# A decoder layer on one core: the second up pair's first product moved behind the first pair's, its weights' sums moved in front of the last output tiles, a later load of the fifth mixed values, and named PSUM banks

## The chip, the cores and the metric

The kernel runs on one core of a Trainium2 chip. The metric is device time in microseconds; the figure for a kernel is the median of its runs. All times in the profile are counted from the start of the span.

TensorE (PE) does the matrix products and loads their stationary operand (PEld, which overlaps). VectorE (DVE) and GpSimd (POOL) do elementwise work, ScalarE (ACT) casts, copies and activations, SyncE (SP) issues the DMAs from one queue, in order.

## The reference

One layer on 1024 positions of width 1024, in float32. Eight heads of sliding-window attention with sinks and eight heads of forgetting attention read the same normalised input; their outputs, side by side, are the mixed values.

```python
mixed = jnp.concatenate([out_a, out_b], axis=-1)       # 1024 x 1024
x = x + jnp.einsum('bse,ed->bsd', mixed, w_out)        # h
hn = rmsnorm(x, mlp_norm_g)
hid = jnp.square(jax.nn.relu(jnp.einsum('bsd,df->bsf', hn, w_up)))   # 4096 wide
x = x + jnp.einsum('bsf,fd->bsd', hid, w_down)
```

## The kernel before

Every float32 product is made of three products in the fast format, of a high and a low part of each operand: high by high, high by low, low by high (`mm`, line 73). `split` makes the parts: a cast on ACT (L77), and the rest by a subtraction on DVE or POOL (L80).

The stages follow each other on PE: input projections and both kinds of attention (to about 430 us, with the first half of the output projection mixed into the tail of attention), the second half of the output projection (`po`, to 468 us), the up product (`pu`, to about 783 us), the down product (`pd`, to the end).

**Output projection.** There are eight output tiles `dt` of 128 columns. Each sums over eight blocks `e` of mixed values. `out_first(dt)` does `e` 0 to 3 while attention still runs and stores the sum with x in DRAM (`part_d`). Once `mix4` to `mix7` are there, `e` 4 to 7 follow: tiles 0 and 4 first, `ahead_of` in the code, partly between the last attention units; then 1, 5, 2, 6, 3, 7. `out_finish(dt)` loads the stored part, adds it on DVE (L981, `h`), stores h, and makes from it slice k = dt % 4 of the seven left operands of the up product: `bh[n]` (high, ACT) and `bl[n]` (low, DVE). The last step of attention, on `mtb`, writes `mix7` in place (L748 and the split of it); `mix3` to `mix6` are loaded from DRAM (L860), one megabyte each.

**Up product.** It is done by pairs `j` of 128-row blocks of w_up, 16 in all, in a scheme of the Strassen kind: seven products per pair instead of eight, in the order `UP = (1, 2, 3, 6, 7, 5, 4)`. Product n of a pair is 12 matmuls: for each k from 0 to 3, wh by `bh[n]`, wh by `bl[n]`, wl by `bh[n]`. Its weights are `wu`, the split of a block of the raw weights (`wur`) or of one of four sums of blocks (`wus`, DVE, L1041 and L1044). For n = 1 the raw block itself is used. For n in (2, 6, 5) DVE makes the low part of `wu`, for the others POOL. Both `bl[n]` for k = 3 and the first pair's `wu` stand on DVE's queue round 470 us.

The code for the order is written as a program in sequence; a scheduler orders each engine's instructions from it, with marks such as `issue_after(x)` (not before x has been issued). SBUF places are named slots ("m3", "r1", "w4"); a new tile in a slot waits until the readers of the old one are done. In front of the up stage,

```python
for dt in (1, 5, 2, 6, 3, 7):
    w = out_weights(dt, 4)
    ps = [bank(f"po{c}") for c in range(2)]
    out_products(ps, w, range(4, 8))
    out_finish(dt, ps)
    if dt == 5:
        with tc.issue_after(part["load"].ins):
            up_load(0)
up_load(1)
```

so the raw weights of pair 0 are issued after the load of tile 5's part, and those of pair 1 behind all tiles.

Of the kernel before, what the change touches and what calls it, by code (L numbers as in the profile page):

```python
# [8 lines left out]
F32 = mybir.dt.float32  # L9
# [7 lines left out]
P = 128  # L17
D = 1024
S = 1024
KT = D // P  # L20
# [35 lines left out]
def hybrid_layer(  # L56
# [15 lines left out]
    def mm(out, lhsT, rhs, start, stop):  # L72
        return nc.tensor.matmul(out, lhsT, rhs, start=start, stop=stop)  # L73
# [70 lines left out]
    def slot(tag, name, shape, dt=F32, pool=None):  # L144
        pool = o[pool or ("zx" if tag in ("w5", "w6") else "zw" if tag[0] == "w" else "zl")]
        return pool.tile([P] + shape, dt, tag=tag, name=name, bufs=1)
# [663 lines left out]
    def heads_b(p):  # L810
        for u in range(8):
            qp, h = (ORDER_END if p == 3 and u > 3 else ORDER_B)[u % 4], u // 4
            unit(lambda: scores_b(p, qp, h), lambda got, qp=qp, h=h: mix_b(got, p, qp, h))
            if u == 1:
                load_c(p, 1)
            if u == DEPTH:
                prep(prep_v, p, 1)
                if p:
                    prep(inverse_to, 6 + 2 * p, dn_b[(p - 1) % 2], 2)
                else:  # L820
                    prep(inverse_a)
            for step in [st.pop(0) for st in splitting if st]:
                step()
            if (p, u) in SPLITS:
                splitting.append(split_mix(SPLITS.index((p, u))))
                splitting[-1].pop(0)()
            if (p, u) in ((2, 4), (3, 1)):
                load_mix(p + 2)
            ahead(p + 1, u)
            fill()  # L830

# [20 lines left out]
        m = mixt[e] = slot(MIX[e], f"mix{e}", [2, S], F32R)  # L852
        mh[e], ml[e] = m[:, 0, :], m[:, 1, :]

    loads = []

    def load_mix(e):
        mix_tiles(e)
        with tc.issue_after(loads[-1]) if e == 4 else nullcontext():
            ld = nc.sync.dma_start(mixt[e].bitcast(F32), mixs_d[e].rearrange("c p s -> p c s"))  # L860
        loads.append(ld.ins)

    nout = [0]

    def out_weights(dt, e0):
        i = nout[0] = nout[0] + 1
        wr = o["zw"].tile([P, 4, P], F32, tag="wor", name="wor", bufs=2)
        nc.sync.dma_start(wr, w_o[dt][:, e0 : e0 + 4, :])
        w = slot(f"w{i % 2}", "wos", [2, 4, P], F32R)
        split(w[:, 0], w[:, 1], wr, nc.scalar, nc.gpsimd)  # L870
        return w[:, 0], w[:, 1]
# [12 lines left out]
    def out_products(ps, w, es):  # L884
        wh, wl = w
        for e in es:
            j = e % 4
            for c in range(2):
                cs = slice(c * 512, (c + 1) * 512)
                mm(ps[c], wh[:, j, :], mh[e][:, cs], j == 0, False)  # L890
                mm(ps[c], wh[:, j, :], ml[e][:, cs], False, False)
            for c in range(2):
                cs = slice(c * 512, (c + 1) * 512)
                mm(ps[c], wl[:, j, :], mh[e][:, cs], False, j == 3)

    def first_banks():
        return [o["pm0"].tile([P, 512], F32, tag=f"m{c}", name=f"po{c}") for c in range(2)]

    def out_first(dt):
        xt = slot(f"w{2 + dt % 2}", "xt", [S])  # L900
        nc.sync.dma_start(xt, xT[dt * P : (dt + 1) * P, :])
        w = out_weights(dt, 0) if dt else first.pop()
        ps = first_banks()
        with paced():
            out_products(ps, w, range(4))
        t = slot("w4", "pc", [S])
        for c in range(2):
            cs = slice(c * 512, (c + 1) * 512)
            nc.scalar.copy(t[:, cs], ps[c])
            nc.gpsimd.tensor_tensor(out=xt[:, cs], in0=xt[:, cs], in1=t[:, cs], op=ALU.add)  # L910
        nc.sync.dma_start(part_d[dt], xt)
# [13 lines left out]
    for p in range(4):  # L925
        heads_b(p)
    fill(True)
    load_mix(6)

    ahead_of = []  # L930
    for dt in (0, 4):
# [43 lines left out]
    def out_finish(dt, ps):  # L975
        t, gain = dt % 4, gm[:, dt : dt + 1]
        h = slot(f"w{2 + dt // 4}", "h", [S]) if dt < 7 else rr
        with tc.issue_after(part["load"].ins) if dt == 7 else nullcontext():
            part["load"] = nc.sync.dma_start(h, part_d[dt])
        for c, cs in enumerate((left, right)):  # L980
            nc.vector.tensor_tensor(out=h[:, cs], in0=ps[c], in1=h[:, cs], op=ALU.add)  # L981
        nc.sync.dma_start(h_d[dt], h)
        if dt < 4:
            h_split(1, t, h[:, left], gain)
            ts = part["t"] = slot("r1", "ts", [4, 512])
            b12 = part["b12"] = slot("w4", "b12", [512])
            nc.scalar.activation(b12, h[:, right], AF.Copy, scale=gain)
            nc.vector.scalar_tensor_tensor(
                out=ts[:, 0], in0=h[:, left], scalar=gain, in1=b12, op0=ALU.mult, op1=ALU.subtract
            )  # L990
            return
        ts, b12 = part["t"], part["b12"]
        h_split(2, t, h[:, left], gain)
        h_split(3, t, h[:, right], gain)
        for i, q, other, op in (
            (1, right, ts[:, 0], ALU.add),
            (2, right, b12, ALU.subtract),
            (3, left, ts[:, 1], ALU.subtract),
        ):
            nc.vector.scalar_tensor_tensor(  # L1000
                out=ts[:, i], in0=h[:, q], scalar=gain, in1=other, op0=ALU.mult, op1=op
            )
        part["rest"] = lambda: sum_splits(ts, t, ((0, 5), (3, 4)))
        sum_splits(ts, t, ((1, 6), (2, 7)))
        if t < 3:
            part.pop("rest")()
# [2 lines left out]
        for i, n in which:  # L1009
            split(bh[n][:, t], bl[n][:, t], ts[:, i], nc.scalar, nc.vector)  # L1010

    for dt, ps, w in ahead_of:
        out_finish(dt, ps)
    pda.close()
    psa.close()
    pm = ctx.enter_context(tc.tile_pool(name="pm", bufs=1, space=PSUM, reuse_waits="tile"))
    bank = lambda name: pm.tile([P, 512], F32, tag="m", name=name, bufs=8)
    raws, up_loads = {}, {}

    def up_load(j):  # L1020
        raws[j] = slot({0: "m3", 1: "m4"}.get(j, f"r{j % 2}"), "wur", [2, KT, P])
        for i in range(2):
            up_loads[j] = nc.sync.dma_start(raws[j][:, i], w_u[j + i * NJ])

    for dt in (1, 5, 2, 6, 3, 7):
        w = out_weights(dt, 4)
        ps = [bank(f"po{c}") for c in range(2)]
        out_products(ps, w, range(4, 8))
        out_finish(dt, ps)
        if dt == 5:  # L1030
            with tc.issue_after(part["load"].ins):
                up_load(0)
    up_load(1)

    def minus(out, a, b, eng=nc.vector):  # L1040
        eng.tensor_tensor(out=out, in0=a, in1=b, op=ALU.subtract)  # L1041
# [1 line left out]
    def plus(out, a, b, eng=nc.vector):  # L1043
        eng.tensor_tensor(out=out, in0=a, in1=b, op=ALU.add)  # L1044

    nw = [4]

    def w_slot(name, shape, dt=F32):
        nw[0] = (nw[0] + 1) % NW
        return slot(f"w{nw[0]}", name, shape, dt)  # L1050

    def up(j):
        if 0 < j < NJ - 1:
            up_load(j + 1)
        raw = raws.pop(j)
        s = slot("m5" if j % 2 == 0 else "m4" if j > 1 else "r1", "wus", [4, 4, P])
        a11, a12, a21, a22 = raw[:, 0, :4], raw[:, 0, 4:], raw[:, 1, :4], raw[:, 1, 4:]
        plus(s[:, 0], a21, a22)  # L1060
        minus(s[:, 1], s[:, 0], a11)
        minus(s[:, 2], a11, a21)
        minus(s[:, 3], a12, s[:, 1])
        src = {1: a11, 2: a12, 3: s[:, 3], 4: a22, 5: s[:, 0], 6: s[:, 1], 7: s[:, 2]}
        m = {}
        for n in UP:
            w = w_slot("wu", [2, 4, P], F32R)
            split(w[:, 0], w[:, 1], src[n], nc.scalar, nc.vector if n in (2, 6, 5) else nc.gpsimd)
            m[n] = bank(f"pu{n}")
            for k in range(4):  # L1070
                mm(m[n], w[:, 0, k], bh[n][:, k], k == 0, False)
                mm(m[n], w[:, 0, k], bl[n][:, k], False, False)
                mm(m[n], w[:, 1, k], bh[n][:, k], False, k == 3)
            if n == 2 and j == 0:
                part.pop("rest")()
            if n == 1:
                u = slot("m1", "u", [4, 512])
                b = slot("m2", "hb", [4, 512])
                nc.scalar.copy(u[:, 0], m[1])
            if n == 2:  # L1080
                plus(b[:, 0], m[2], u[:, 0])
            if n == 6:
                plus(u[:, 1], m[6], u[:, 0])
            if n == 7:
                plus(u[:, 2], m[7], u[:, 1])
# [283 lines left out]
```

## Time and profile before

| | us |
|---|---|
| median of 3 runs | 1092.21 |
| lowest, highest | 1091.84, 1093.93 |
| the profiled execution | 1091.76 |
| its span | 1090.0 |
| mean granted clock of TensorE | 0.998 |
| busy: PE | 1074.8 (99%) |
| busy: PEld | 931.5 (85%) |
| busy: DVE | 783.0 (72%) |
| busy: ACT | 572.3 (53%) |
| busy: POOL | 382.2 (35%) |

The span runs from the first to the last instruction; the device time of the same execution lies 1.8 us above it. In the rows of waits, the engine and line that waited and the one waited for are followed by the total in us, the count and the longest. A row of the timeline gives the start, the duration, the engine, the line and operation, the tile written and those read, and in brackets the idle time before it and what ended it. Matmuls overlap, so the distance from start to start is what counts for PE.

### The profile page before, as it was taken

To read this page: it belongs to the slowest core of one execution; us is meant where nothing else is said; L and a number is where in the kernel's file an instruction comes from. 1 tells how busy PE (TensorE), PEld (TensorE's weight loads), DVE (VectorE), ACT (ScalarE), POOL (GpSimd) and SP (SyncE) were. 2 spreads that over 40 slices of the span, in tenths; PEclk is the share of its full clock that TensorE was granted. 3 is DMA by queue.
4 is the path that set the end of the run, shared out by engine and by line. 5 is a ranking of instruction groups with operands and counts; after the bars stand their busy time and mean duration, and the time that the engine had idled before them with its cause. 6 is when DMAs were issued, how large, how long until landed. Compare 5 with 4: busy or idle time off the path is not lost.

```text
span 1090.0 us, 15620 instructions
## 1 busy us (share of the span) xinstructions
PE 1074.8 (99%) x5492; PEld 931.5 (85%) x5492; DVE 783.0 (72%) x1319; ACT 572.3 (53%) x1022; POOL 382.2 (35%) x350
## 2 busy tenths in 40 slices
PE   9999999999999999989999999999999999999998
PEld 8999999999988887868888888888888888888886
DVE  8377677766766786998686869665675876664395
ACT  5558588776767765554545453443533433333331
POOL 4572524546455662323232232332222222231100
PEclk9999999999999999999999999999999999999999
DMA  9401212324757664754445533443998885665523
GB/s 295 154 23 53 65 43 69 109 84 144 240 182 244 198 202 133 251 193 146 183 174 193 182 146 136 148 170 145 335 390 311 307 298 209 241 224 185 172 88 115
DMA packets 96222, 195.67 MB, mean 180 GB/s; under 512 B 7392, under 2 KB 19856, under 8 KB 96144
## 3 DMA queue, kind: packets, MB, share of 16 engines
q1 hardware_dynamic: 95856, 194.54, 51.5%
q8 instruction: 43, 0.70, 0.3%
q14 instruction: 35, 0.29, 0.1%
q10 hardware_dynamic: 288, 0.15, 0.0%
HBM read 141.61 MB, written 53.04 MB: 179 GB/s over the span
## 4 chain that ended last, share of the span: by engine, by line
PE 83%; DVE 7%; DMA 3%; issue 3%; POOL 2%; ACT 1%; SPq 0%; POOLq 0%; DVEq 0%; ACTq 0%
PE pd L73 28%; PE pu L73 27%; PE ps L73 10%; PE po L73 4%; PE qps L73 3%; PE spb L73 2%; PE pvb L73 2%; PE tpb L733 2%; PE sp L73 1%; PE pv L73 1%; PE tpa L558 1%; DVE bl L80 1%; DMA mix_d<-mtb 1%; DVE ts L1000 1%; DVE bl L971 1%
## 5 line engine op out<-in xcount | busy, mean ns | idle before, releaser
L73 PE MATMUL pd<-hx,wx 128*128 128x512 f32 (+1 forms) x1350 | 304.9, 388 | 0.0
L73 PEld LDWEIGHTS pd<-hx,wx 128*128 128x128 f32 x1350 | 252.6, 188 | 52.3
L73 PE MATMUL pu<-bh,wu 128*128 128x512 f32 x896 | 278.2, 391 | 0.9 <-ACT wu L77 0.6
L73 PEld LDWEIGHTS pu<-bh,wu 128*128 128x128 f32 x896 | 168.9, 189 | 37.2 <-ACT wu L77 0.9
L73 PE MATMUL ps<-w,x 128*128 128x384 f32 (+1 forms) x960 | 195.8, 342 | 0.3 <-ACT z L453 0.3
L73 PE MATMUL pu<-bl,wu 128*128 128x512 f32 x448 | 174.9, 391 | 1.8 <-DVE bl L80 1.8
L73 PEld LDWEIGHTS ps<-w,x 128*128 128x128 f32 x960 | 165.0, 188 | 3.8 <-ACT z L453 0.6
L77 ACT CAST hx<-hr 128x1024 fp32r<-128x1024 f32 x56 | 59.0, 1054 | 174.7 <-PE pd L73 170.4
L80 POOL TENSOR_TENSOR wx<-wda,wx 128x1024 fp32r<-128x1024 f32 x24 | 64.7, 2697 | 196.2 <-ACT wx L77 192.9
L80 DVE TENSOR_TENSOR hx<-hr,hx 128x1024 fp32r<-128x1024 f32 x56 | 74.8, 1344 | 71.0 <-ACT hx L77 71.0
L73 PEld LDWEIGHTS pu<-bl,wu 128*128 128x128 f32 x448 | 84.5, 189 | 20.3 <-DVE bl L80 2.2
L73 PE MATMUL po<-mix,wos 128*128 128x512 f32 x384 | 94.5, 394 | 0.3 <-ACT wos L77 0.3
L80 POOL TENSOR_TENSOR wu<-wus,wu 128x512 fp32r<-128x512 f32 x32 | 46.4, 1451 | 125.0 <-ACT wu L77 125.0
L73 PEld LDWEIGHTS po<-mix,wos 128*128 128x128 f32 x384 | 70.5, 188 | 14.8 <-ACT wos L77 1.1
L80 POOL TENSOR_TENSOR wu<-wur,wu 128x512 fp32r<-128x512 f32 x32 | 43.6, 1362 | 89.7 <-ACT wu L77 89.6
L77 ACT CAST wu<-wus 128x512 fp32r<-128x512 f32 x64 | 38.5, 618 | 63.3 <-PE pu L73 57.2
L1041 DVE TENSOR_TENSOR ht<-hb 128x512 f32<-128x512 f32 x32 | 22.9, 756 | 63.2 <-ACT hb L1096 63.2
L697 ACT ACTIVATE sb<-sb,nmb 128x128 f32<-128x128 f32 (+3 forms) x64 | 49.8, 779 | 29.7 <-DVE nmb L692 29.4
L77 ACT CAST wx<-wda 128x1024 fp32r<-128x1024 f32 x56 | 58.5, 1049 | 8.3 <-DMA wda<-in_w_d_dram 8.3
L80 POOL TENSOR_TENSOR w<-wr,w 128x384 fp32r<-128x384 f32 (+1 forms) x47 | 49.9, 1071 | 31.9 <-ACT w L77 18.1
L396 DVE TENSOR_TENSOR ptl<-tpb,pth 128x512 fp32r<-128x512 f32 (+1 forms) x80 | 49.6, 631 | 16.0 <-ACT pth L395 15.4
L733 PE MATMUL tpb<-ident,sb 128*128 128x128 f32 x288 | 47.5, 275 | 3.8 <-DVE ptl L396 3.3
(205 smaller groups left out, 1822.6 us busy)
## 6 DMA issues: line engine op xcount, KB each, us to landing
wda<-in_w_d_dram SPq DMA_DIRECT2D x34, 1024.0 KB, 9.5
hr<-hid_d SPq DMA_DIRECT2D x56, 512.0 KB, 6.5
wur<-in_w_u_dram SPq DMA_DIRECT2D x32, 512.0 KB, 4.4
hid_d<-ht SPq DMA_DIRECT2D x16, 1024.0 KB, 4.3
hid_d<-hb SPq DMA_DIRECT2D x16, 768.0 KB, 3.6
mix<-mixs_d SPq DMA_DIRECT2D x7, 1024.0 KB, 6.3
wr<-in_w_b_dram SPq DMA_DIRECT2D x32, 192.0 KB, 2.5
xq<-in_x_dram SPq DMA_DIRECT2D x8, 512.0 KB, 5.5
```

What stands on the lines that cost most here:

```text
L73: return nc.tensor.matmul(out, lhsT, rhs, start=start, stop=stop)
L77: hi_eng.copy(hi, src)
L80: lo_eng.tensor_tensor(out=lo, in0=src, in1=hi.bitcast(F32), op=ALU.subtract)
L396: nc.vector.tensor_tensor(out=lo[:, cols], in0=pt[:, cols], in1=hi[:, cols].bitcast(F32), op=ALU.subtract)
L558: nc.tensor.transpose(tp[:, hh * P : (hh + 1) * P], pts[hh // 2][:, hh % 2, c0 : c0 + P], ident)
L697: nc.scalar.activation(pr[:, :nk], pr[:, :nk], AF.Exp, scale=-1.0, bias=nm[:, c : c + 1], accum_out=dn_b[p % 2][:, h, i : i + 1] if p < 3 ...
L733: nc.tensor.transpose(tp[:, c0 : c0 + P], probs[qi][:, kb * P : (kb + 1) * P], ident)
L971: nc.vector.scalar_tensor_tensor(out=lo, in0=src, scalar=gain, in1=hi.bitcast(F32), op0=ALU.mult, op1=ALU.subtract)
L1000: nc.vector.scalar_tensor_tensor(out=ts[:, i], in0=h[:, q], scalar=gain, in1=other, op0=ALU.mult, op1=op)
L1041: eng.tensor_tensor(out=out, in0=a, in1=b, op=ALU.subtract)
```

## The change

Five things are changed:

1. The raw weights of pairs 0 and 1 (`up_load(0)`, `up_load(1)`, two loads of 512 KB each) are issued right behind the load of `mix6`. Pair 1's are put in slot m2 instead of m4.
2. The four sums of pair 0 (`up_sum(0)`) and the split of the weights of product 1 of pairs 0 and 1 (`up_weights`) are written in front of the six last output tiles.
3. Product 1 of pair 1 runs right behind product 1 of pair 0.
4. `mix4` is loaded in `out_first(2)`, behind that tile's load of x, instead of in the head units.
5. Each PSUM bank has a name of its own, used in turn, with one skipped in pair 1; before, one name had eight buffers. `hb` of pair 0 uses slot m0.

```diff
-            if (p, u) in ((2, 4), (3, 1)):
-                load_mix(p + 2)
+            if (p, u) == (3, 1):
+                load_mix(5)
...
         w = out_weights(dt, 0) if dt else first.pop()
+        if dt == 2:
+            with tc.issue_after(ld.ins):
+                load_mix(4)
...
-    load_mix(6)
+    last_mix = load_mix(6)
...
-        raws[j] = slot({0: "m3", 1: "m4"}.get(j, f"r{j % 2}"), "wur", [2, KT, P])
+        raws[j] = slot({0: "m3", 1: "m2"}.get(j, f"r{j % 2}"), "wur", [2, KT, P])
...
+    def up_weights(n, src):
+        w = w_slot("wu", [2, 4, P], F32R)
+        split(w[:, 0], w[:, 1], src, nc.scalar, nc.vector if n in (2, 6, 5) else nc.gpsimd)
+        return w
+
+    with tc.issue_after(last_mix.ins):
+        up_load(0)
+        up_load(1)
+    for dt, ps, w in ahead_of:
+        out_finish(dt, ps)
+    up_sums[0] = up_sum(0)
+    up_ahead = [up_weights(1, up_sums[0][1]), up_weights(1, raws[1][:, 0, :4])]
...
+    def bank(name):
+        nbank[0] += 1
+        return pm.tile([P, 512], F32, tag=f"m{nbank[0] % 8}", name=name, bufs=1)
...
     for dt in (1, 5, 2, 6, 3, 7):
...
-        if dt == 5:
-            with tc.issue_after(part["load"].ins):
-                up_load(0)
-    up_load(1)
...
+            if n == 1 and j == 1:
+                m[n] = second.pop()
+            else:
+                w = up_ahead.pop(0) if n == 1 and j == 0 else up_weights(n, src[n])
+                m[n] = bank(f"pu{n}")
+                up_products(n, w, m[n])
+            if n == 1 and j == 0:
+                second.append(bank("pu1"))
+                up_products(1, up_ahead.pop(), second[0])
             if n == 2 and j == 0:
                 part.pop("rest")()
+            if n == 2 and j == 1:
+                nbank[0] += 1
```

How the instructions move. On DVE at the end of attention, before (`mtb` is the last attention value, `h` the sums of the first output tiles):

```order
L748 TENSOR_TENSOR mtb_5765<-pvb_2506,mtb_5765 64x256
L80 TENSOR_TENSOR mix7_4344<-mtb_5765,mix7_4344 64x256
L748 TENSOR_TENSOR mtb_5814<-pvb_2506,mtb_5814 64x256
L80 TENSOR_TENSOR mix7_4344<-mtb_5814,mix7_4344 64x256
L981 TENSOR_TENSOR h_5867<-po0_5721,h_5867 128x512
```

and after the change:

```order
L748 TENSOR_TENSOR mtb_5765<-pvb_2506,mtb_5765 64x256
L80 TENSOR_TENSOR mix7_4344<-mtb_5765,mix7_4344 64x256
L1022 TENSOR_TENSOR wus_5904<-wur_5867 128x512
L1019 TENSOR_TENSOR wus_5904<-wur_5867 128x512
L1019 TENSOR_TENSOR wus_5904<-wus_5904,wur_5867 128x512
L748 TENSOR_TENSOR mtb_5814<-pvb_2506,mtb_5814 64x256
L1019 TENSOR_TENSOR wus_5904<-wur_5867,wus_5904 128x512
L80 TENSOR_TENSOR mix7_4344<-mtb_5814,mix7_4344 64x256
L980 TENSOR_TENSOR h_5873<-po0_5721,h_5873 128x512
```

Three sums of pair 0's weights now stand ahead of the last `mtb` add, and the fourth ahead of the last piece of `mix7`.

On PE, where the up product begins, before (the last row of output tile 7, then products 1 and 2 of pair 0):

```order
L73 MATMUL po1_6140<-mix7_4344,wos_6136 128x512
L73 MATMUL pu1_6191<-bh1_5852,wu_6188 128x512
L73 MATMUL pu1_6191<-bl1_5853,wu_6188 128x512
L73 MATMUL pu1_6191<-bh1_5852,wu_6188 128x512 x2
```

```order
L73 MATMUL pu1_6191<-bh1_5852,wu_6188 128x512
L73 MATMUL pu2_6210<-bh2_5854,wu_6207 128x512
L73 MATMUL pu2_6210<-bl2_5855,wu_6207 128x512
L73 MATMUL pu2_6210<-bh2_5854,wu_6207 128x512 x2
L73 MATMUL pu2_6210<-bl2_5855,wu_6207 128x512
```

and after (`pu1_6194` is pair 0's product 1, `pu1_6207` pair 1's):

```order
L73 MATMUL po1_6154<-mix7_4344,wos_6150 128x512
L73 MATMUL pu1_6194<-bh1_5852,wu_5909 128x512 x2
L73 MATMUL pu1_6194<-bl1_5853,wu_5909 128x512
L73 MATMUL pu1_6194<-bh1_5852,wu_5909 128x512 x2
L73 MATMUL pu1_6194<-bl1_5853,wu_5909 128x512
L73 MATMUL pu1_6194<-bh1_5852,wu_5909 128x512 x2
L73 MATMUL pu1_6207<-bh1_5852,wu_5912 128x512
L73 MATMUL pu1_6207<-bl1_5853,wu_5912 128x512
L73 MATMUL pu1_6194<-bl1_5853,wu_5909 128x512
L73 MATMUL pu1_6194<-bh1_5852,wu_5909 128x512
L73 MATMUL pu1_6207<-bh1_5852,wu_5912 128x512 x2
```

The product of pair 1 follows, and `pu2` comes only behind it; two products of `pu1_6194` stand earlier, within output tile 3.

On SP behind the load of `mix6`, before:

```order
L860 DMA mix6_5719<-mixs_d_74 128x2x1024
L982 DMA h_d_76<-h_5867 128x1024
L982 DMA h_d_76<-h_5878 128x1024
L868 DMA wor_5999<-in_w_o_dram 128x512
L868 DMA wor_6041<-in_w_o_dram 128x512
L979 DMA h_5934<-part_d_75 128x1024
L979 DMA h_5976<-part_d_75 128x1024
L1023 DMA wur_5996<-in_w_u_dram 128x1024 x2
```

and after:

```order
L857 DMA mix6_5719<-mixs_d_74 128x2x1024
L1016 DMA wur_5867<-in_w_u_dram 128x1024 x2
L1016 DMA wur_5870<-in_w_u_dram 128x1024 x2
L981 DMA h_d_76<-h_5873 128x1024
L981 DMA h_d_76<-h_5884 128x1024
L864 DMA wor_6013<-in_w_o_dram 128x512
```

The raw weights of both pairs now come before the stores of h and the loads of the last tiles.

More of the change, by code (lines that the diff above doesn't have):

```diff
@@ L853, in mix_tiles @@
         mh[e], ml[e] = m[:, 0, :], m[:, 1, :]
-    loads = []
     def load_mix(e):
         mix_tiles(e)
-        with tc.issue_after(loads[-1]) if e == 4 else nullcontext():
-            ld = nc.sync.dma_start(mixt[e].bitcast(F32), mixs_d[e].rearrange("c p s -> p c s"))
-        loads.append(ld.ins)
+        return nc.sync.dma_start(mixt[e].bitcast(F32), mixs_d[e].rearrange("c p s -> p c s"))
     nout = [0]
@@ L900, in out_first @@
         xt = slot(f"w{2 + dt % 2}", "xt", [S])
-        nc.sync.dma_start(xt, xT[dt * P : (dt + 1) * P, :])
+        ld = nc.sync.dma_start(xt, xT[dt * P : (dt + 1) * P, :])
         w = out_weights(dt, 0) if dt else first.pop()
+        if dt == 2:
+            with tc.issue_after(ld.ins):
+                load_mix(4)
         ps = first_banks()
@@ L1010, in sum_splits @@
             split(bh[n][:, t], bl[n][:, t], ts[:, i], nc.scalar, nc.vector)
[L1012 to L1018, printed above, removed]
+    raws, up_loads, up_sums = {}, {}, {}
     def up_load(j):
-        raws[j] = slot({0: "m3", 1: "m4"}.get(j, f"r{j % 2}"), "wur", [2, KT, P])
+        raws[j] = slot({0: "m3", 1: "m2"}.get(j, f"r{j % 2}"), "wur", [2, KT, P])
         for i in range(2):
             up_loads[j] = nc.sync.dma_start(raws[j][:, i], w_u[j + i * NJ])
[L1025 to L1029, printed above, removed]
-        if dt == 5:
-            with tc.issue_after(part["load"].ins):
-                up_load(0)
-    up_load(1)
     def minus(out, a, b, eng=nc.vector):
@@ L1044, in plus, with up_sum @@
         eng.tensor_tensor(out=out, in0=a, in1=b, op=ALU.add)
[L1046 to L1056, printed above, removed]
+    def up_sum(j):
         raw = raws.pop(j)
@@ L1063, in up, with w_slot @@
         minus(s[:, 3], a12, s[:, 1])
-        src = {1: a11, 2: a12, 3: s[:, 3], 4: a22, 5: s[:, 0], 6: s[:, 1], 7: s[:, 2]}
+        return {1: a11, 2: a12, 3: s[:, 3], 4: a22, 5: s[:, 0], 6: s[:, 1], 7: s[:, 2]}
+    nw = [4]
+    def w_slot(name, shape, dt=F32):
+        nw[0] = (nw[0] + 1) % NW
+        return slot(f"w{nw[0]}", name, shape, dt)
+    def up_weights(n, src):
+        w = w_slot("wu", [2, 4, P], F32R)
+        split(w[:, 0], w[:, 1], src, nc.scalar, nc.vector if n in (2, 6, 5) else nc.gpsimd)
+        return w
@@ new lines, in hybrid_layer @@
+    with tc.issue_after(last_mix.ins):
[5 more added lines that the diff above has]
+    up_ahead = [up_weights(1, up_sums[0][1]), up_weights(1, raws[1][:, 0, :4])]
+    pda.close()
+    psa.close()
+    pm = ctx.enter_context(tc.tile_pool(name="pm", bufs=1, space=PSUM, reuse_waits="tile"))
+    nbank = [0]
+    def bank(name):
+        nbank[0] += 1
+        return pm.tile([P, 512], F32, tag=f"m{nbank[0] % 8}", name=name, bufs=1)
@@ new lines, in hybrid_layer, with up_products, up @@
+    for dt in (1, 5, 2, 6, 3, 7):
+        w = out_weights(dt, 4)
+        ps = [bank(f"po{c}") for c in range(2)]
+        out_products(ps, w, range(4, 8))
+        out_finish(dt, ps)
+    def up_products(n, w, ps):
+        for k in range(4):
+            mm(ps, w[:, 0, k], bh[n][:, k], k == 0, False)
+            mm(ps, w[:, 0, k], bl[n][:, k], False, False)
+            mm(ps, w[:, 1, k], bh[n][:, k], False, k == 3)
+    second = []
+    def up(j):
+        if 0 < j < NJ - 1:
+            up_load(j + 1)
+        src = up_sums.pop(0) if j == 0 else up_sum(j)
@@ L1065, in up @@
         m = {}
         for n in UP:
[L1067 to L1073, printed above, removed]
+            if n == 1 and j == 1:
[4 more added lines that the diff above has]
+                up_products(n, w, m[n])
@@ L1074, in up @@
+            if n == 1 and j == 0:
+                second.append(bank("pu1"))
+                up_products(1, up_ahead.pop(), second[0])
             if n == 2 and j == 0:
                 part.pop("rest")()
+            if n == 2 and j == 1:
+                nbank[0] += 1
             if n == 1:
                 u = slot("m1", "u", [4, 512])
-                b = slot("m2", "hb", [4, 512])
+                b = slot("m2" if j else "m0", "hb", [4, 512])
                 nc.scalar.copy(u[:, 0], m[1])
```

## The prediction

> **What bounds the kernel now.** I read the shares of the engines first (TensorE, PE, is busy 99% of the span, so only PE's lost time counts), then the waits of PE, then the windows round the place where the waits lie, then the rows of the engines that end them. PE's waits from 400 us on:
>
> ```profile
> PE pu L73 <- DVE bl L80: 1.8, 1, 1.8
> PE tpb L733 <- DVE ptl L396: 1.5, 1, 1.5
> PE pu L73 <- ACT wu L77: 0.6, 1, 0.6
> ...
> PE pu L73 <- ACT bh L970: 0.3, 1, 0.3
> ```
>
> Three of these stand at the start of the up product (`pu`): 1.8 + 0.6 + 0.3 = 2.7 us. The windows (busy time and count of PE, PEld, DVE, ACT, POOL; then the clock, the DMA share and GB/s) show what else is lost there:
>
> ```profile
> 460.00:470.00 10.00, 10.00 (x46) 8.28 (x45) 10.00 (x16) 5.53 (x9) 1.55 (x1) 1.00 0.65 232
> 470.00:480.00 10.00, 9.10 (x38) 6.65 (x36) 10.00 (x16) 6.25 (x11) 1.34 (x2) 1.00 0.87 341
> 480.00:490.00 10.00, 8.15 (x29) 6.32 (x30) 10.00 (x13) 4.32 (x8) 5.16 (x3) 0.86 0.17 54
> 600.00:700.00 100.00, 100.00 (x439) 82.11 (x438) 80.61 (x108) 43.80 (x55) 28.07 (x22) 1.00 0.44 157
> ```
>
> Undisturbed, PE does 439 products in 100 us, 0.2278 us each. From 470 to 480 it does 38 and from 480 to 490 it does 29, where 44 would fit. VectorE (DVE) is busy for all 30 us from 460 to 490: it sets the pace there. The matmuls on `pu` alone, then PE's windows of 3.41 us:
>
> ```profile
> 468.40:500.00 31.60, 28.65 (x115) 22.48 (x116) 4.59 (x7) 0.59 (x1) 0.95 0.44 166
> ```
>
> ```profile
> 483.86:487.27 3.41, 1.65 (x8) 1.00 0.16 56
> 487.27:490.68 3.41, 3.41 (x10) 0.50 0.00 0
> ...
> 418.85:422.26 3.41, 1.91 (x15) 1.00 0.51 197
> ```
>
> In 31.60 us 31.60/0.2278 = 139 products fit and 115 are done: 24 are lost, 24 x 0.2278 = 5.5 us. Of these 2.7 are the waits, 3.41 x 0.5 = 1.7 is the half clock after the gap, and the remaining 1.1 is refilling behind each wait (a wait of 0.28 us costs more than 0.28 from start to start: in the rows below, the product at 473.13 follows one at 472.46 by 0.67, not 0.23).
>
> ```profile
> 472.46 0.39 PE L73 MATMUL pu<-bh,wu 128*128 128x512 f32 x1
> 473.13 0.50 PE L73 MATMUL pu<-bh,wu 128*128 128x512 f32 x1 [0.28 <-ACT bh L970]
> 474.25 0.49 PE L73 MATMUL pu<-bh,wu 128*128 128x512 f32 x1 [0.62 <-ACT wu L77]
> 483.62 0.39 PE L73 MATMUL pu<-bl,wu 128*128 128x512 f32 x1
> 485.77 0.50 PE L73 MATMUL pu<-bl,wu 128*128 128x512 f32 x1 [1.76 <-DVE bl L80]
> ```
>
> **The sums in front of the last tiles.** Why DVE is late stands in its own rows:
>
> ```profile
> 449.51 1.37 DVE L80 TENSOR_TENSOR wu<-wur,wu 128x512 fp32r<-128x512 f32 x1 [1.86 <-ACT wu L77]
> 450.81 1.28 DVE L981 TENSOR_TENSOR h<-po,h 128x512 f32<-128x512 f32 x2
> 452.00 0.68 DVE L1044 TENSOR_TENSOR wus<-wur 128x512 f32<-128x512 f32 x1
> 452.60 0.68 DVE L1041 TENSOR_TENSOR wus<-wur 128x512 f32<-128x512 f32 x1
> 471.63 1.28 DVE L981 TENSOR_TENSOR h<-po,h 128x512 f32<-128x512 f32 x2
> 474.64 1.48 DVE L971 SCALAR_TENSOR_TENSOR bl<-h,vt,bh 128x512 fp32r<-128x512 f32 x1
> 477.30 0.74 DVE L971 SCALAR_TENSOR_TENSOR bl<-rr,vt,bh 128x512 fp32r<-128x512 f32 x1
> 480.55 1.78 DVE L1000 SCALAR_TENSOR_TENSOR ts<-rr,vt,ts 128x512 f32<-128x512 f32 x1
> 482.26 3.45 DVE L80 TENSOR_TENSOR bl<-ts,bh 128x512 fp32r<-128x512 f32 x2
> ```
>
> DVE stands 1.86 us waiting for `wu`, whose raw weights were issued only at 443.90 (SP's row below), and then has four sums of pair 0 (two are shown) that start 0.60 us apart, 4 x 0.60 = 2.4 us, among the tiles' sums. Both leave this stretch. DVE therefore comes 1.86 + 2.4 = 4.3 us earlier: the values of the last pair of output tiles (k = 3) of `bl1` end at 476.12 - 4.3 = 471.8, of `bl2` at 478.04 - 4.3 = 473.7, and the last pair of rows at 485.71 - 4.3 = 481.4.
>
> PE needs them later than before, since pair 1's first product (12 x 0.2278 = 2.73 us) comes between. By the new order, ten products stand between the end of the output tiles (468.6, plus 0.45 for two products of pair 0 moved ahead) and the first use of `bl1` at k = 3: 468.6 + 0.45 + 2.28 = 471.3. Then 26 more until `bl2` at k = 3: 477.2. The last was wanted at 483.85 (0.23 behind 483.62); the two early waits, in which 0.44 + 0.89 = 1.3 us are lost from start to start, fall away, and 2.73 come on: 485.2. So the margins are -0.5, +3.5 and +3.8 us. The first can cost 0 (the new order also puts the tile's sums earlier than an even shift does) to 0.9 with refilling; I take 0.4. With no gap of 1.76 us the half clock goes as well.
>
> `wu` for both first products is cast by ACT in front of the tiles and finished by POOL there, so the 0.62 wait for ACT's cast has no place left. POOL:
>
> ```profile
> 435.59 3.46 POOL L80 TENSOR_TENSOR wos<-wor,wos 128x512 fp32r<-128x512 f32 x2 [18.32 <-ACT wos L77]
> 474.27 1.29 POOL L80 TENSOR_TENSOR wu<-wus,wu 128x512 fp32r<-128x512 f32 x1 [10.69 <-ACT wu L77]
> 479.96 1.83 POOL L80 TENSOR_TENSOR wu<-wur,wu 128x512 fp32r<-128x512 f32 x1 [4.39 <-ACT wu L77]
> ...
> 483.44 1.72 POOL L80 TENSOR_TENSOR wu<-wur,wu 128x512 fp32r<-128x512 f32 x1
> ```
>
> It was idle for 18 us before 435.59; two pieces of 1.3 to 1.7 us from about 433 put `wos` of tile 1 back to about 436.0: 0 to 0.5 us late for the third kind of product, I take 0.3.
>
> **The loads.** The 1 MB load of `mix6` is issued at 422.35 and lands 4.9 us later, at 427.3; the four 512 KB loads now follow it directly (SP's rows, then the loads by group with the median time from issue to landing).
>
> ```profile
> 422.35 0.37 SPq L860 DMA_DIRECT2D mix<-mixs_d  x1
> ...
> 443.90 0.90 SPq L1023 DMA_DIRECT2D wur<-in_w_u_dram  x2
> ```
>
> ```profile
> mix<-mixs_d SPq DMA_DIRECT2D x1, 1024.0 KB, 4.9
> wur<-in_w_u_dram SPq DMA_DIRECT2D x4, 512.0 KB, 6.7
> ```
>
> ```profile
> 430.24 0.42 DVE L748 TENSOR_TENSOR mtb<-pvb,mtb 64x256 f32<-64x256 f32 x1 [1.29 <-ACT mtb L747]
> 431.12 0.42 DVE L80 TENSOR_TENSOR mix<-mtb,mix 64x256 fp32r<-64x256 f32 x1 [0.47 <-ACT mix L77]
> 433.49 2.05 DVE L981 TENSOR_TENSOR h<-po,h 128x512 f32<-128x512 f32 x3 [1.95 <-PE po L73]
> ```
>
> In the window from 470 to 480 the queues moved 341 GB/s at a share of 0.87, 392 GB/s at full use, so 512 KB (0.524 MB) take 1.3 us: pair 0's two halves land near 428.6 and 429.9 and pair 1's by 432.5 (estimates from these two rows). On SP only two h stores, a weight load and the next part loads stand behind the four issues, all needed after 440. On DVE three sums now stand ahead of the last `mtb` add, the fourth ahead of the last piece of `mix7`: with both halves in by 429.9 the add goes from 430.24 to 429.9 + 3 x 0.6 = 431.7, the hi values come near 432.6 and the lo ones near 433.4.
>
> ```profile
> 429.58 5.69 PE L73 MATMUL po<-mix,wos 128*128 128x512 f32 x24
> ```
>
> PE begins at 429.58 with 12 products on `mix6` and 6 on the left half of `mix7`, and reaches the right half at 429.58 + 18 x 0.2278 = 433.7: 1.1 us to spare, and DVE had 1.95 us of idle time there. Cost 0; the cover is gone if the second half lands after about 430.9.
>
> **The mixed values.** `mix4`'s megabyte is taken out of a crowded stretch near 324 us and issued near 347. It is used after 400, so its lateness costs nothing. What it may free is a stall of PE behind `rd`, whose buffer waits for a store in that queue (first row; the second is the tail's).
>
> ```profile
> 336.81 0.66 PE L324 MATMUL ptq<-ident,qkb 128*128 128x128 f32 x4 [0.25 <-DVE rd L581]
> 420.62 1.17 PE L733 MATMUL tpb<-ident,sb 128*128 128x128 f32 x7 [1.50 <-DVE ptl L396]
> ```
>
> PE's order changes in small ways from 334 to 425 us, while the tail of attention goes at the pace of the softmax on DVE and ACT (1.50 idle at 420.62). Either sign is open, up to some 1.0 of those 1.50; I take -0.3, the stall of 0.25 with its refilling. The window 418.85 to 422.26 above, with 1.91 of 3.41 busy, kept its clock; the one with 1.65 busy lost the next. If the tail's idle time grows by 0.3, it may cost 1.7 us.
>
> **The banks.** No wait of PE for a bank is among the rows above; pair 1's product holds one for some 84 products, 19 us, and the numbering skips it once. 0; against it stands only a late evacuation by DVE, which is earlier than before.
>
> **Sum.** -5.5 + 0.4 + 0.3 + 0 - 0.3 = -5.1 against the profiled execution's 1091.76 (span 1090.0): 1086.7. The three runs' median is 1092.21, 0.45 above it, so the middle of both ways of counting, 1087.0, is the prediction.
>
> [...]
>
> **Rivals.** B: the lateness moves on. The rows at 480.55 (1.78) and 482.26 (1.73 each) run beside POOL's rows from 479.96 to 485.16, and the same forms take 0.74 and 0.68 with POOL idle. Three of POOL's four rows stay, so if these stretch the tiles' sums too, the margins of 3.5 and 3.8 us are eaten; a stall of over 1.7 us in one window then keeps the half clock. Lost then: about 1.5 + 1.7 of the 5.5, so 1086.7 + 3.2 = 1089.9.
>
> C, slower: DVE, which works in order, stands with the last attention values behind the three sums. If pair 0's second half lands at T > 430.9, PE loses T - 430.9, and 1.7 more for the clock once that exceeds about 1.7. It cancels the gain at T = 434.2 and gives slower by 0.2% at T = 436.4, 14 us after `mix6`'s issue. The four `wur` loads above took 6.7 us in the median, all four in one queue, which speaks against it; landing at 437, it would be 1086.7 + 6.1 + 1.7 = 1094.5.
>
> D: the gain doesn't come out at the end, because attention's tail, in its new order, loses what the transition gains (stalls grow by 3 us and the clock halves): about 1091.5.
>
> E: the half clock isn't bound to the gap. If it comes back after a shorter one, in whatever window, -5.1 + 1.7 = -3.4: 1088.4. [...]
>
> **How the numbers follow.** My sum 0.61, B 0.17, C 0.06, D 0.10, E 0.06. A measurement of this kernel can't tell less than 0.2%, 2.2 us, from no change, so faster means below 1090.0: mine, E, and a third of B, 0.73. The rest of B and most of D make "same", 0.18; C and a little of D are slower, 0.09. The low end takes the margins and the attention at their best (no 0.4, no 0.3, -1.0 for -0.3) by the profiled execution's counting, 1086.7 - 1.4 = 1085.3; the high end takes in B and part of D, 1091.0.
>
> **What would show it.** After the change: no wait of `pu` for `bl`, `wu` or `bh` above 0.4 us; the clock at 1.00 in 480 to 500; 135 or more `pu` products in the 31.6 us behind the last output tile; DVE's h sums of tile 5 at 449 and not 450.8; the three `wus` sums near 430 and the last `mtb` add before 432. Wrong would be: a wait of `po` for `mix` near 434; a `pu` wait for `bl` of over 1.5 us; or a span from 334 to 425 us that is longer by more than 1 us.

## The result and the profile after

| | median us | lowest, highest | runs |
|---|---|---|---|
| before | 1092.25 | 1090.50, 1093.93 | 20 |
| after the change | 1090.41 | 1087.32, 1092.57 | 20 |

The ratio is 0.998, with a 95% interval of 0.9972 to 0.9987: 1.8 us faster by the medians, a third of the 5.2 us that was forecast. The time lies inside the range given, at its upper end. The one profiled execution that came with the result is the fastest of the twenty (1087.32 us, span 1085.6), so it shows the forecast's case, and not the usual one. PE's waits from 400 us on in it:

```profile
PE tpb L733 <- DVE ptl L396: 1.0, 1, 1.0
PE po L73 <- ACT mix L77: 0.9, 1, 0.9
PE po L73 <- ACT wos L77: 0.8, 1, 0.8
```

The three waits of `pu` are gone. In the output tiles the wait for `mix` is new, and the one for `wos` was shorter before:

```profile
PE po L73 <- ACT wos L77: 0.3, 1, 0.3
```

The windows on all engines at the start of the up product, and then the 31.6 us behind the last output tile for `pu` alone:

```profile
470.00:480.00 10.00, 10.00 (x46) 8.28 (x45) 9.31 (x12) 6.83 (x13) 2.79 (x2) 1.00 0.39 152
480.00:490.00 10.00, 10.00 (x46) 8.29 (x45) 10.00 (x17) 3.00 (x6) 2.15 (x1) 1.00 0.09 29
```

```profile
470.23:501.83 31.60, 31.60 (x140) 26.18 (x140) 5.19 (x8) 1.15 (x2) 1.00 0.26 96
```

140 products where there were 115, and 46 in each 10 us where there were 38 and 29: the transition is clean. What the change costs stands 40 us earlier, in DVE's and PE's rows:

```profile
431.01 0.69 DVE L1022 TENSOR_TENSOR wus<-wur 128x512 f32<-128x512 f32 x1 [3.02 <-DMA wur<-in_w_u_dram]
431.62 0.69 DVE L1019 TENSOR_TENSOR wus<-wur 128x512 f32<-128x512 f32 x1
432.22 0.68 DVE L1019 TENSOR_TENSOR wus<-wus,wur 128x512 f32<-128x512 f32 x1
432.94 0.42 DVE L748 TENSOR_TENSOR mtb<-pvb,mtb 64x256 f32<-64x256 f32 x1
433.39 0.69 DVE L1019 TENSOR_TENSOR wus<-wur,wus 128x512 f32<-128x512 f32 x1
434.11 0.42 DVE L80 TENSOR_TENSOR mix<-mtb,mix 64x256 fp32r<-64x256 f32 x1
```

```profile
428.61 4.33 PE L73 MATMUL po<-mix,wos 128*128 128x512 f32 x18
433.85 1.94 PE L73 MATMUL po<-mix,wos 128*128 128x512 f32 x6 [0.91 <-ACT mix L77]
436.58 9.79 PE L73 MATMUL po<-mix,wos 128*128 128x512 f32 x40 [0.79 <-ACT wos L77]
```

DVE stands for 3.0 us until pair 0's raw weights are in at 431.0; the last `mtb` add, which PE needs for the right half of `mix7`, comes at 432.94 and not at 431.7. PE does the 18 products that it can and waits. The second wait, for `wos` of tile 1, goes back to the same sums. On DVE the sums of the first output tile (`h`) stand behind them; on ACT `bh` waits for the first of these, and the cast of `wos` comes after `bh`:

```profile
434.57 1.89 DVE L980 TENSOR_TENSOR h<-po,h 128x512 f32<-128x512 f32 x3
```

```profile
435.29 0.72 ACT L969 ACTIVATE bh<-h,vt 128x512 fp32r<-128x512 f32 x1 [0.33 <-DVE h L980]
435.92 0.60 ACT L77 CAST wos<-wor 128x512 fp32r<-128x512 f32 x1
```

To compare executions, the span is cut at four starts on PE: the first product of the output projection (A begins), the first product on `mix6` (B), tile 1's first second-half product (C), and pair 2's first product. Between the first two cuts stand 599 matmuls before and after. From pair 2 to the end it is 577.7 to 578.2 us in every execution, and none of PE's waits above is for a bank, so part 5, the banks, shows no cost. What lies ahead of A differs by up to 4.3 us from execution to execution of whatever kernel. What is called a half clock here is 3.41 us at a granted clock of 0.50, as from 487.27 to 490.68 in the first execution of before: 3.41 x 0.5 = 1.7 us of PE's work (an estimate from that row; in C, the two executions of before differ by 1.53 us).

| execution | A us | B us | C us | half clock in A to C |
|---|---|---|---|---|
| before | 101.81 | 5.99 | 76.66 | in C |
| before, a second one | 102.05 | 5.98 | 75.13 | none |
| after | 100.08 | 7.97 | 71.28 | none |
| after, a second one | 101.53 | 8.82 | 73.31 | at 329 (A) and at 438 (B, C) |

### The profile page after: what moved, and what is told of

Same layout as the page of the kernel before. It is cut to its first block, busy times and chain, and to the rows that moved or that the text cites. A ratio compares the mean times of both kernels' runs of the same rounds, so it can differ in the third digit from the quotient of the medians.

```text
span 1085.6 us, 15576 instructions
## 1 busy us (share of the span) xinstructions
PE 1071.7 (99%) x5492; PEld 930.4 (86%) x5492; DVE 776.1 (71%) x1319; ACT 573.3 (53%) x1022; POOL 381.9 (35%) x350
## 4 chain that ended last, share of the span: by engine, by line
PE 86%; DVE 5%; DMA 3%; issue 2%; ACT 1%; POOL 1%; SPq 0%; DVEq 0%; POOLq 0%; ACTq 0%
PE pu L73 28%; PE pd L73 28%; PE ps L73 11%; PE po L73 7%; PE spb L73 3%; PE pvb L73 2%; PE tpb L733 2%; PE sp L73 1%; PE pv L73 1%; PE tpa L558 1%; DMA xq<-in_x_dram 1%; DMA wur<-in_w_u_dram 1%; DVE x L207 1%; DMA mixn<-rd_d 1%; PE ptk L324 1%
## 5 line engine op out<-in xcount | busy, mean ns | idle before, releaser
L80 DVE TENSOR_TENSOR hx<-hr,hx 128x1024 fp32r<-128x1024 f32 x56 | 72.4, 1302 | 71.5 <-ACT hx L77 71.5
```

What stands on the lines that cost most here:

```text
L80: lo_eng.tensor_tensor(out=lo, in0=src, in1=hi.bitcast(F32), op=ALU.subtract)
```

## The experiments

Each was run in turn with the kernel before on the same chip; ratios are to it.

**The changed kernel again.** No edit.

> The changed kernel once more, for a second profiled execution. Its one profile (1087.3 us) is the fastest of 20 runs with a median of 1090.4; the transition into the up product had gained 5.4 us in it, and 2.0 us were lost between the first output tiles and tile 1 (0.9 waiting for mix, 0.8 for wos) behind sums that stood until 430.99 for the second half of pair 0's weights. Theory 1 (the weights land at a time that differs from run to run, and DVE's queue passes it on): median 1090 to 1091, and a slower execution shows the landing later than 431 and a longer po wait for mix, up to 3 us more and 1.7 for the clock. Theory 2 (attention in its new order differs from run to run): the same median, po waits as before, and the beginning of the last output stage later than 428.6 by the missing 3 us. Theory 3 (the gain at the up product comes only in some runs): pu waits for bl return.

1090.57 us median of 12 (1087.91 to 1093.45), ratio 0.9983 (0.9970 to 0.9996). Its profiled execution took 1092.82 us. DVE's row of the first sum, PE's longest wait there, and PE's windows around both gaps:

```profile
434.43 0.69 DVE L1022 TENSOR_TENSOR wus<-wur 128x512 f32<-128x512 f32 x1 [3.90 <-DMA wur<-in_w_u_dram]
```

```profile
PE po L73 <- ACT mix L77: 1.8, 1, 1.8
```

```profile
435.03:438.45 3.42, 1.64 (x7) 1.00 0.04 16
438.45:441.86 3.41, 3.14 (x9) 0.50 0.35 141
325.81:329.22 3.41, 1.73 (x10) 1.00 1.00 381
329.22:332.64 3.42, 3.42 (x10) 0.50 1.04 365
```

The bracketed counts are PE's products; behind them stand the clock, the DMA share and GB/s. The wait for `mix` has doubled and the clock halves behind it; `pu` has no wait but 0.3 for `wu`. This is the price that the forecast gave to its rival C, wait and half clock both. The second half clock, near 329, stands behind a gap that every kernel here has. The weights landed 3.9 to 4.1 us behind `mix6` in both executions, so the landing itself doesn't vary as theory 1 had it. What varies is PE: its first product on `mix6` came 1.67 us behind that landing in one execution and 0.69 in the other.

**The sums behind the h sums of tiles 0 and 4.**

```diff
-    up_sums[0] = up_sum(0)
+    with tc.issue_after(part["add"].ins):      # last h sum of tile 4
+        up_sums[0] = up_sum(0)
```

> The changed kernel with the four sums of pair 0's weights behind the h sums of output tiles 0 and 4 on DVE, so that the last attention values no longer stand behind the weights' landing. Theory 1: faster than the changed kernel by 2 us at the least run and by 3 to 4 in the median, 1086 to 1087.5, with a smaller spread. Theories 2 and 3: 1.5 to 2 us faster at most and the spread of 5 us stays.

1090.2 us median of 10 (1087.64 to 1092.07), ratio 0.9978 (0.9967 to 0.9989). B is 5.95 us: the wait for `mix` is gone, as theory 1 says, but the time misses its 1086 to 1087.5. C is 75.41: the 2.4 us of sums now delay the tiles' sums, and the lateness comes out at the up product as a wait of `pu` for `bh`, with a half clock behind it:

```profile
PE pu L73 <- ACT bh L969: 1.7, 1, 1.7
```

```profile
471.28 0.62 ACT L77 CAST wu<-wus 128x512 fp32r<-128x512 f32 x1 [2.22 <-issue]
471.80 0.72 ACT L969 ACTIVATE bh<-h,vt 128x512 fp32r<-128x512 f32 x1
```

ACT stands 2.2 us before a cast of `wu`, and `bh` is behind it in its queue. (What the cast stands for isn't named; it starts when the store of h that empties a slot has landed, at 471.2. In the changed kernel the same cast stands 1.64 us, and the trace names that store.)

**The parts at the up product without the later `mix4`.** The two places of `load_mix` as before, all else as in the change.

> The changed kernel with mix4 loaded in the head units as before; the orders of all engines up to the last output tiles are those of the kernel before, and the parts at the up product are those of the change. Theory 1: no faster than the changed kernel, 1090.5 to 1091.5 (attention's 1.0 us, which the one profile shows as gained, is given back). Theory 2: 1086.5 to 1088.5, since attention goes as before. Theory 3: near 1090.5, as the changed kernel.

1094.89 us median of 12, ratio 1.0020 (1.0010 to 1.0031): slower, and a miss for all three. The undo was not clean: the scheduler now put two of the sums ahead of the last but one `mtb` add.

```profile
PE pvb L73 <- DVE mtb L748: 5.2, 1, 5.2
```

```profile
432.24 0.69 DVE L1024 TENSOR_TENSOR wus<-wur 128x512 f32<-128x512 f32 x1 [3.76 <-DMA wur<-in_w_u_dram]
432.85 0.68 DVE L1021 TENSOR_TENSOR wus<-wur 128x512 f32<-128x512 f32 x1
433.57 0.42 DVE L748 TENSOR_TENSOR mtb<-pvb,mtb 64x256 f32<-64x256 f32 x1
```

So PE could not even write the last `pvb` for 5.2 us. A is 108.33 us, where the kernel before has 101.81 and 102.05: two sums one place further ahead in the queue cost more than the rest of the change gains.

**`mix4` later and nothing else.** Part 4 of the change in the kernel before.

> The kernel before with mix4 loaded in the second output tile's first half and nothing else. Theory 1 and 3: 1091 to 1092.3 (attention 0 to 1 us shorter). Theory 2: 1093 to 1095, or a wider spread than the kernel before.

1090.55 us median of 11 (1088.88 to 1093.66), ratio 0.9981 (0.9969 to 0.9992). This part alone moves the median by as much as the whole change; every theory had it wrong. Its profiled execution has the half clock near 330, a C of 75.06 as before, and PE's wait of 1.7 for `bl` at the up product.

**The sums right behind the last piece of `mix7`.**

```diff
-    up_sums[0] = up_sum(0)
+    with tc.issue_after(last_lo[0]):           # low part of mix7's last piece
+        up_sums[0] = up_sum(0)
```

> The changed kernel with the first three sums of pair 0's weights right behind the last piece of mix7 on DVE (and the fourth behind one h sum), so that the last attention values no longer wait for the weights' landing, and the sums still stand in DVE's idle time. Theory 1 (the transition gains what the forecast said, and the wait of mix7 behind the weights' landing, 2.0 to 2.9 us on PE and 1.7 to 2.0 more when the clock halves behind it, takes it back): the time from the first product on mix6 to pair 2's first product, 79.25 and 82.13 us in two executions of the changed kernel, falls to 77 to 77.5; median 1087 to 1088.3. Rival (the lateness moves on, as with the sums behind the h sums, where it became a wait of 1.7 for bh and a half clock): 79 to 81.5 us there, median 1089.5 to 1090.5.

1089.24 us median of 6 (1087.39 to 1090.32), ratio 0.9962 (0.9949 to 0.9975). Faster than the change by the medians, with intervals that overlap, but less than theory 1 said: B is 7.55, and C 72.52 with a half clock at its start. The wait for `mix` became one for `wos`, of tile 1:

```profile
PE po L73 <- ACT wos L77: 1.9, 1, 1.9
```

```profile
434.11 0.62 ACT L77 CAST wu<-wur 128x512 fp32r<-128x512 f32 x1 [1.97 <-DMA wur<-in_w_u_dram]
435.89 0.72 ACT L970 ACTIVATE bh<-h,vt 128x512 fp32r<-128x512 f32 x1 [1.16 <-DVE h L981]
436.52 1.12 ACT L77 CAST wos<-wor 128x512 fp32r<-128x512 f32 x2
```

```profile
432.79 1.26 DVE L1023 TENSOR_TENSOR wus<-wur 128x512 f32<-128x512 f32 x1 [1.20 <-DMA wur<-in_w_u_dram]
433.98 0.68 DVE L1020 TENSOR_TENSOR wus<-wur 128x512 f32<-128x512 f32 x1
434.58 0.68 DVE L1020 TENSOR_TENSOR wus<-wus,wur 128x512 f32<-128x512 f32 x1
435.18 0.68 DVE L981 TENSOR_TENSOR h<-po,h 128x512 f32<-128x512 f32 x1
```

ACT, too, stands for the early weights (1.97 us), but what ends last in front of `bh` and `wos` is the h sum, 1.16 us later: on DVE it stands behind three sums that could begin only when the weights were in.

**The same with `mix4` early.**

> The same, with mix4 loaded in the head units as before the change: the orders up to the last output tiles are those of the kernel before on PE. Theory 1, with mix4's own gain of 2 us (90.96 against 89.0 us from the second first-half tile to the first product on mix6): 2 us slower than the kernel with the sums behind mix7, 1089 to 1090.3, and 2 to 3 us faster than the kernel before. Rival: no faster than 1091.5.

1091.04 us median of 11, ratio 0.9983 (0.9973 to 0.9993), and A is 101.99: 1.8 us slower than its pair with the later `mix4`. The size of that part is confirmed; the gain on the kernel before is 1.5 us, less than the 2 to 3 expected, since the wait for `wos` (2.3) is there. This time it is not the landing: the weights were in at 432.80, before DVE wanted them. Two of the sums took 1.78 and 1.77 us instead of 0.68, beside POOL's rows of `wu`, and the h sum came late behind them:

```profile
434.20 1.78 DVE L1022 TENSOR_TENSOR wus<-wur 128x512 f32<-128x512 f32 x1
435.91 1.77 DVE L1022 TENSOR_TENSOR wus<-wus,wur 128x512 f32<-128x512 f32 x1
437.61 0.68 DVE L983 TENSOR_TENSOR h<-po,h 128x512 f32<-128x512 f32 x1
```

```profile
433.83 3.30 POOL L80 TENSOR_TENSOR wu<-wur,wu 128x512 fp32r<-128x512 f32 x2 [14.54 <-ACT wu L77]
```

**Pair 1's first product back in its place.** Part 3 undone in the changed kernel.

> The changed kernel with pair 1's first product back behind all of pair 0's; its weights are still made ahead. If the product is needed as cover (2.73 us) for DVE: a pu wait for bl or bh of 1 to 2 us returns, with a half clock in most executions, median 1091.5 to 1093. If the early sums alone carry the gain: 1090.2 to 1091, as the changed kernel.

1089.99 us median of 10, ratio 0.9975 (0.9964 to 0.9985): not told apart from the changed kernel by its time. In the trace C is 73.67 and not 71.28, both without a half clock, with waits of `pu` for DVE's `wu` of 1.0 in all. As cover the product is worth 2.4 us in one execution; the waits are for `wu` and not for `bl` as expected.

**Pair 0's raw weights ahead of `mix6`.** With the sums behind `mix7`.

> As the kernel with the sums behind mix7, with pair 0's raw weights also issued ahead of mix6's load, so that they are in before DVE wants them. Theory 1: no further gain beyond 0.5 us if the sums fall into DVE's idle time either way, unless mix6 lands later than 429.6 and PE waits for it; 1087 to 1088.5. Rival: as the kernel with the sums behind mix7, whatever that gives.

1089.67 us median of 5, ratio 0.9966 (0.9954 to 0.9978). `mix6` now lands behind two more loads, and PE waits 1.3 us for it. The weights are in early, but two sums take 1.79 and 1.77 us beside POOL again, and PE waits 0.8 us for `wos`. Nothing is won by that order.

**Sums and casts both out of the way.** As with the sums behind `mix7`, and on ACT the casts of `wu` behind the casts of `wos` of tiles 1 and 5 (`with tc.issue_after(wos_cast)` around `up_ahead`).

> The changed kernel with both waits for the landing of the early weights taken from in front of the output tiles: the sums stand behind the last piece of mix7 on DVE, and the casts of wu for both first products stand behind the casts of wos of tiles 1 and 5 on ACT (with the sums alone moved, ACT stood until 435.3 for pair 1's weights and PE waited 1.9 us for wos). Theory 1 (queues that stand for the weights' landing take back the gain): no wait of po for mix or wos over 0.4 us; from the first product on mix6 to tile 1's first product 6.0 to 6.3 us, from there to pair 2's first product 71.3 to 72, together 77.3 to 78.3; median 1087 to 1088.3, so 4 to 5 us faster than the kernel before. Rival (the lateness moves on to ACT or DVE in the tiles): 79 to 81 us, median 1089 to 1090.5.

1089.21 us median of 12 (1085.77 to 1092.26), ratio 0.9962 (0.9949 to 0.9975): 3.4 us below the kernel before by the medians, 1.2 to 1.4 below those of the changed kernel. The lowest time of the study is among its runs. The sizes were too good again: B is 6.76 and C 73.31, so their sum and the median are the rival's. Against the sums behind `mix7` alone (1089.24) the casts' place shows no difference in time.

```profile
PE po L73 <- ACT wos L79: 1.1, 1, 1.1
PE tpb L736 <- DVE ptl L398: 1.0, 1, 1.0
PE pu L73 <- DVE wu L82: 0.5, 1, 0.5
```

What is left is one step removed: `wos` stands on ACT behind `bh`, `bh` waits for the h sum, and that stands on DVE behind sums that waited 0.97 us for the weights.

**The casts alone.** The changed kernel with that edit on ACT only.

> The changed kernel with the casts of wu behind the casts of wos of tiles 1 and 5, the sums in front of the last attention values as in the change. Theory 1: the wait for mix stays (0.9 to 1.8 us), the wait for wos falls from 0.8 to 0.3; from the first product on mix6 to tile 1's first product 7.0 to 8.5; median 1089 to 1090.5. Rival (the casts alone matter): 6.0 to 6.5 us there, median 1087.5 to 1088.5.

1090.47 us median of 12, ratio 0.9977 (0.9964 to 0.9990). The wait for `mix` stays at 1.8, that for `wos` is 0.2 (0.3 in the second execution of the changed kernel, without the edit), and B is 8.87. The casts are no part of B: with them out of the way ACT stands all the longer for the h sum.

```profile
438.13 0.72 ACT L971 ACTIVATE bh<-h,vt 128x512 fp32r<-128x512 f32 x1 [1.50 <-DVE h L982]
```

**The kernel before again.**

> The kernel before, for a second profiled execution. If the half clock that two of the profiled executions show near 330 us (0.50 there, in the kernel with only mix4 moved and in one of the changed kernel, behind a gap that every kernel has) is a matter of where the gap falls in time and not of the change: this execution may or may not show it, with the same gap. In either case 90.9 to 91.1 us from tile 1's first-half products to the first product on mix6, and 81.0 (no half clock) or 82.7 us (half clock) from there to pair 2's first product.

1091.82 us; A and B as before. The same wait for `bl`, 1.7 us, this time without a half clock:

```profile
PE pu L73 <- DVE bl L80: 1.7, 1, 1.7
```

```profile
483.25:486.67 3.42, 2.24 (x10) 1.00 0.36 128
486.67:490.08 3.41, 2.86 (x12) 1.00 0.02 5
```

## Why the prediction was wrong, point by point

Of the signs that the prediction named, three came: no wait of `pu` above 0.4 us, the clock at 1.00, 140 products. Three did not: the h sums of tile 5 came at 450.34 and not at 449, the first `wus` sum at 431.01, the last `mtb` add at 432.94. And a sign of being wrong came: a wait of `po` for `mix` near 434.

**The 5.5 us at the up product: the mechanism was right, and the sum counted too much.** Waits and refilling went as worked out: C is 3.9 us shorter than in the second execution of before, which kept its clock. The other 1.5 to 1.7 us were the half clock. The prediction took it as a fixed term of the kernel ("with no gap of 1.76 us the half clock goes as well"); the second execution shows the same wait (1.7 us) at a clock of 1.00. It belongs to some executions, before and after. The 0.4 for `bl1` did not come; no such wait is in the profile after.

**The loads and the sums ahead of the last attention values: the failed step.** "In the window from 470 to 480 the queues moved 341 GB/s [...] so 512 KB (0.524 MB) take 1.3 us", T = 429.9, cost 0. Pair 0's second half landed 3.9 to 4.1 us behind `mix6`, and not 2.6. The trace of before held a sign of it: its two loads of pair 0, issued at 443.90 and 444.38, landed at 448.3 and 451.1, 2.75 us apart, and I had used a mean rate instead. (From issue to landing the second took 6.7 us there, and 7.9 after the change.) Counted from PE's first product on `mix6` this is 2.1 to 3.3 us (the table below) and not the forecast's 0.3, since PE also came to `mix6` sooner behind its landing, 0.7 to 1.8 us against 2.3 before. Rival C was thus under way in both traced executions of the change. That the lateness is passed on one to one is confirmed by four executions in which the sums stand ahead of `mix7`; the second column is from PE's first product on `mix6` to the landing:

| execution | landing behind us | B us |
|---|---|---|
| after | 2.38 | 7.97 |
| without the second product | 3.13 | 8.72 |
| after, a second one | 3.23 | 8.82 |
| casts later | 3.28 | 8.87 |
| sums behind the h sums | 2.11 | 5.95 |

B minus the landing is 5.59 in the first four to 0.01 us, and with the sums out of the way (last row) it doesn't follow. Against B of 5.98 before, the cost is 2.0 to 2.9 us. For the wait that rival C names, its point of decision was right: PE is back at the right half of `mix7` 2.86 us behind the landing in all four, so that wait begins when the landing is 1.3 us behind the first product (430.9 against 429.58 in the prediction). But B grows from 0.4 us on, because of a second path that the prediction put at nothing: the first h sum, which stands on DVE behind the fourth sum and the last piece of `mix7`. Counted from PE's first product on `mix6`, it came 3.91 us behind it before the change and 5.95 after, and in all thirteen traces tile 1's first product starts 1.99 to 2.07 us behind that sum, by way of `bh` and `wos` on ACT. Of the 2.0 to 2.9 us, 1.1 to 2.0 are the wait for `mix` with its refilling, and 0.9 is this path.

**POOL's 0.3 us for `wos`.** It did not come: PE's waits for `wos` in the changed kernel, 0.8 us in one execution and 0.3 in the other, are for ACT, by the path of the h sum just named; the kernel before has 0.3 of it too. The casts of `wu`, which stand in front of `bh` on ACT, are not the cause: with them moved, B minus the landing is the same 5.59.

**`mix4`: -0.3 was too small by a factor of six.** A went from 101.8 and 102.05 to 100.1 in three executions with `mix4` later and no half clock there, and to 100.9 in a fourth; a fifth, with pair 0's weights ahead of `mix6`, has 101.7, of which 1.3 is the wait for `mix6`. Named in the traces are the stalls behind `rd` (0.65 from start to start, gone), one of `spb` at 370 (0.53, gone) and the tail's wait for `ptl`:

```profile
PE tpb L733 <- DVE ptl L396: 1.5, 1, 1.5
PE spb L73 <- DVE nmb L692: 0.7, 2, 0.5
PE ptq L324 <- DVE rd L581: 0.3, 1, 0.3
```

before, from 327 us to the end of A, and after (the `spb` wait of 0.5 stands just ahead of A in both):

```profile
PE tpb L733 <- DVE ptl L396: 1.0, 1, 1.0
PE spb L73 <- DVE nmb L692: 0.5, 1, 0.5
```

These make some 1.3 us (0.42, 0.41 and 0.49, from start to start beyond the usual distance); the rest of the 1.8 lies in small pieces between products in another order, and was not traced to one cause. The prediction saw either sign open up to 1.0 and took the nearest stall.

**Together.** Without any half clock: A -1.9, B +2.0 to +2.9, C -3.9, so -2.9 to -3.8. The medians give 1.8. The mean granted clock can bear only a part of the difference: it is 0.9985 over the runs of the kernel before, and 0.9980 over the twelve later runs of the changed kernel, 0.0005 of 1090 us or 0.5 us; over the first 20 runs of the changed kernel it is 0.9987, which gives nothing. With two traced executions of each kernel, and up to 4.3 us of difference ahead of A, the rest stays open. In the traces, half to three quarters of the gain at the up product went on the waits 40 us earlier; the median that is left is about that of `mix4` alone, whose runs have a mean clock of 0.9991.

**The rivals.** C is what happened, at a part of its price. B and D came near the measured time for other reasons: no `pu` wait for `bl` returned, and attention gained instead of losing. E is half right: the half clock did come back in other windows, at 329 and 438 us. PE was busy there for 1.73 and 1.64 of the 3.41 us in front of each, and for 1.65 in front of the one before the change.

## What to carry to other kernels

Work put into an idle place of an engine costs nothing only if its own inputs are there and nothing that is wanted soon stands behind it: on DVE here, whose rows came in the order of its queue, the early sums that waited for a load (3.02 us in the first execution of the change) made everything behind them wait as well, one to one (B minus the landing is 5.59 us in four executions). When the wait that shows has been moved out of the way, the next one shows: here `mix` from DVE first, then `wos` from ACT, which was waiting for DVE as well. So follow a wait back until an engine is reached that stands for nothing else. Take the landing of a load from the same load's rows in the trace, each of them, not from a mean rate (here two landings 2.75 us apart, where the mean rate gave 1.3). And where executions differ, compare stages cut at the same instruction, over more than one execution, before a term such as a half clock is booked as the kernel's own.

## What the runs showed of the hardware

Nine of the thirteen traced executions have a half clock between 300 and 510 us, two of them a second one. Where the rows above have its edges (487.27, 438.45 and 329.22), it lasts 3.41 to 3.42 us at 0.50. PE's products start further apart in it: in the first execution of before, six take 2.56 us from 488.09 to 490.65, 0.43 us each and not 0.2278. Counted by slices of 5 us, 5 us times what the clock lacks of 1.00, each half clock comes to 1.70 or 1.75 us; in the kernel with two sums ahead of the last but one `mtb` add it is 3.45, twice as much, behind the wait of 5.2 us.

Longer waits of PE than 1.5 us, from 400 us on, and the granted clock of the slices at and behind them:

| execution | PE's wait | clock, slices of 5 us |
|---|---|---|
| before | 1.8, `pu` for `bl` | 0.73, 0.93 from 485 |
| before, a second one | 1.7, `pu` for `bl` | 1.00, 1.00 from 485 |
| `mix4` later and nothing else | 1.7, `pu` for `bl` | 1.00, 1.00 from 485 |
| without the second product | 1.7, `po` for `mix` | 1.00, 1.00 from 430 |
| sums behind the h sums | 1.7, `pu` for `bh` | 0.88, 0.77 from 470 |
| after, a second one | 1.8, `po` for `mix` | 0.84, 0.81 from 435 |
| casts later | 1.8, `po` for `mix` | 0.78, 0.88 from 435 |
| sums behind `mix7` | 1.9, `po` for `wos` | 0.77, 0.88 from 435 |
| the same, `mix4` early | 2.3, `po` for `wos` | 1.00, 0.66 from 435 |
| without the later `mix4` | 5.2, `pvb` for `mtb` | 0.81, 0.50 from 430 |

The waits of 1.5 us for `ptl` between 415 and 430 us, in the four executions that load `mix4` early (both of before among them), left the clock at 1.00. Waits of 1.7 us went with a half clock in one execution and without it in three, and what decides between the two was not shown. In the kernel before, the wait for `bl` went with a half clock in one execution (1.76 us) and without it in the other (1.7). The gap near 325, which all the kernels have (two waits, 1.18 and 0.51 us, in the first execution of before), went with a half clock in four of the thirteen executions.
